# A state space, attention and feed-forward block on one core: oT's split behind the last head, half of w_out's split among the gates, four banks for two sets of transposes, and another order ahead of the state space

## Chip, core and metric

The kernel runs on one core of a Trainium2 chip. The metric is device time in microseconds (us), the median of several runs. A run of this kernel is one launch that reads all inputs from HBM and writes the whole output.

Five things work side by side on a core: TensorE (PE, matrix products and transposes into PSUM banks), VectorE (DVE), ScalarE (ACT), GpSimd (POOL), and the DMA queues, most of them filled by SyncE (SP). Each engine works through its own list in order. Semaphores tie the lists together.

## The reference, cut to what matters

One layer on 512 tokens of width 1024, in fp32:

```
n1 = rmsnorm(x, g_mix);  z = n1 @ w_in
y_ssm = s5_mixer(z[:, 0:512], ...)             # diagonal state space, 32 groups, gelu, glu
y_nsa = nsa_mixer(q = z[:, 512:1024], kv = z[:, 1024:1792], gates, ...)
merge = sigmoid(z[:, 1816:])
mixed = merge[:, :1024] * (y_ssm @ w_br_ssm) + merge[:, 1024:] * (y_nsa @ w_br_nsa)
h = x + mixed @ w_out
h = h + conv_ffn(rmsnorm(h, g_ffn), ...)
h = h + sigmoid(rmsnorm(h, g_ple) @ w_ple_gate) * (p @ w_ple_proj)
return rmsnorm(h, g_final)
```

The attention has 8 heads in two groups, each head with a compressed branch, a selected branch and a window branch.

## The kernel before, in words

**Split products.** PE takes its operands in a format that keeps fewer bits than fp32. So each fp32 operand is split into a high half and a low half: `split` (L86) copies to the high half on ACT (`copy`, L84) and subtracts on DVE or POOL (`tt`, L61). `mm3` (L90 to L93) then issues three matmuls, high by high (L91), by low (L92, L93). A weight comes by `wload` (L191): a DMA on SP into a raw buffer `wr` (three in turn), a copy `wh` on ACT, a subtraction `wl`. `wh` and `wl` have two buffers each, unless `keep` names a place of its own. In this kernel a projection of 128 columns is 24 matmuls of 128x512 (`proj`, L202; a bank `pj`).

**Transposes and banks.** `to_t` (L160) transposes a normed tile by PE (L168), four transposes to a bank, and reads each bank with ACT (the high half, L171) and DVE (the low half, `stt`, L72). Its argument `tags` says which of the PSUM banks it takes: there are two each of `acc`, `s`, `t`, `o`, and `?` stands for acc and o in turn (`either`, L180). A transpose into a bank waits until the last readers of that bank are done.

**Order.** In three parts the order is written out (`manual_schedule`); elsewhere a scheduler lays the recorded instructions out, led by the order in which the code records them and by `tc.issue_after(x)`, which holds instructions behind x.

**The state space stage.** The four projections u (columns 0 to 511 of w_in), the query projections 0 to 3 (`queries`), and four quarters of the state space (`ssm_quarter`, L725) share PE. DVE makes the tables of the state space: the powers PR and PI (L584 to L598), nr, den, kr and ki (L601 to L614), bb (L706 to L711), then for each quarter the products z (L735, with POOL making x beside them) and the scans. In the code before, PR to ki are recorded ahead of the u projections, behind `trig_at`, so that DVE's list has them between the `wl` of the second and third u weight. `wbps` (L755) are the transposes of Z, `wps` (L763) products of their result, `cps` (L634) transposes of C.

**Attention.** For 16 units (a head and a branch, L1118), `scores` makes `sps`, ACT its exponential `pr`, `transposed` (L1040) turns `pr` on PE into `ptp`, and `split` makes `ph` (ACT) and `pl` (DVE); `values` (L1049) multiplies by them into `ops`, and at the end of a head ACT copies `otmp` and DVE adds `oT`. Between them PE gets fillers (L1082): the gates (`pj` with L937's tanh) and the state space's branch products `br` with `t1b` (L1071). When the last head is done, `for _ in fill: pass` (L1134) records what is left of the fillers, some six gates. Then comes `oS`, the split of oT in four parts (L1144), w_br_nsa's products `br` from oS (L1155), `mTh` and `mTl`, and w_out: two halves of 512 columns, four loads each, `w0h`/`w0l` (POOL) and `w1h`/`w1l` (DVE) (L1172). 

**Norms 2 and 3.** The output product `wo` gives `hres`; for each pair of row tiles `to_t` makes n2h and n2l (L1202), the operands of the feed-forward products `ua` and `ub`. Behind the feed-forward part, norm 3 has two pairs too: `transposed(0, ...)` with the tags "tt??" and `transposed(1, ...)` with "tttt" (L1556), for the gating products `pg` (L1568).

Of the kernel before, what the change touches and what calls it, by code (L numbers as in the profile page):

```python
# [18 lines left out]
P = 128  # L19
# [26 lines left out]
def hybrid_kernel(ctx: ExitStack, tc: tile.TileContext, A, out):  # L46
# [36 lines left out]
    def copy(o, a):  # L83
        S.activation(o, a, AF.Copy)  # L84
# [90 lines left out]
    def last(engine):  # L175
        return next(i for i in reversed(nc.cur_bb.bb.instructions) if i.engine == engine)
# [54 lines left out]
    pP = sP.enter_context(pool("ssm_prep", 1, "right"))  # L231
    prow = pP.tile([NPAIR, 3, P], F32, name="prow")
# [3 lines left out]
    braw = pP.tile([P, 2, NPAIR, 16], F32, name="braw")  # L236
# [245 lines left out]
    with tc.manual_schedule(engines={mybir.EngineType.PE, mybir.EngineType.Activation, mybir.EngineType.DVE,  # L482
# [86 lines left out]
        trig_at = last(mybir.EngineType.DVE)  # L569
        rho_at = last(mybir.EngineType.Pool)  # L570
# [10 lines left out]


    behind = ExitStack()
    behind.enter_context(tc.issue_after(trig_at))  # L584
# [17 lines left out]
    nr, den, kr, ki = (st(n) for n in ("nr", "den", "kr", "ki"))  # L602
    ts(nr, PR[:, :, 1], -1.0, None, ADD)
    tt(den, lre, lre, MUL)
    tt(pt, aim, aim, MUL)
    tt(den, den, pt, ADD)
    V.reciprocal(den, den)
    tt(kr, nr, lre, MUL)
    tt(pt, PI[:, :, 1], aim, MUL)
    tt(kr, kr, pt, ADD)  # L610
    tt(kr, kr, den, MUL)
    tt(ki, PI[:, :, 1], lre, MUL)
    tt(pt, nr, aim, MUL)
    tt(ki, ki, pt, SUB)  # L614
    tt(ki, ki, den, MUL)
    shb = [P, NPAIR, 16]
    bt = st("bt", shb)
# [56 lines left out]
    tab_at = last(mybir.EngineType.Pool)  # L674
# [20 lines left out]
    ud = pud.tile([4, P, L, NCH], F32, name="ud")  # L695
    for ct in range(4):
        un = pw.tile([P, L, NCH], F32, name="un", tag="mg")
        copy(un, proj(ct * P, w=uw[ct] if ct < 2 else None).rearrange("p (c j) -> p j c", j=L))
        nc.sync.dma_start(ud[ct], un)
        for j in range(L):  # L700
            n = L - 1 - j
            nc.sync.dma_start(Uc[32 * n:32 * n + 32, 4 * ct:4 * ct + 4], ud[ct, :, j].rearrange("(a c) k -> c a k", c=32))


    with tc.issue_after(last(mybir.EngineType.DVE)):
        tt(bb[:, 0], braw[:, 0], krb, MUL)  # L706
        tt(bt, braw[:, 1], kib, MUL)
        tt(bb[:, 0], bb[:, 0], bt, SUB)
        tt(bb[:, 1], braw[:, 0], kib, MUL)
        tt(bt, braw[:, 1], krb, MUL)  # L710
        tt(bb[:, 1], bb[:, 1], bt, ADD)  # L711
# [11 lines left out]
    for t in SR:  # L723
        G.memset(t[:, :, 0:1], 0.0)
    def ssm_quarter(q, afters):  # L725
# [24 lines left out]

        WB = []
        for i, z in enumerate((Zr, Zi)):
            ps = bank("t", "wbps")
            for b in range(4):
                PE.transpose(ps[:, b * P:(b + 1) * P], z[:, b].rearrange("p j g c -> p (j g c)"), ident)  # L755
# [59 lines left out]
        for j in range(L):  # L815
            o = [yps[32 * b:32 * b + 32, j * NCH:(j + 1) * NCH] for b in range(4)]
            for b in range(4):
                PE.matmul(o[b], tz[:, b, 32 * j:32 * j + 32], Uc[:, 4 * q + b], start=True, stop=False)
            for x, s, last in ((Xr, sr[0], False), (Xi, sr[1], True)):
                for b in range(4):  # L820
                    PE.matmul(o[b], x[:, b, j + 1].rearrange("p g c -> p (g c)"), s[:, b], start=False, stop=last)
# [8 lines left out]
    with tc.issue_after(tab_at):  # L830
        G.tensor_copy(W2d, W2[:, 0:1].to_broadcast([P, 2, HD]))
# [3 lines left out]
    with tc.issue_after(tab_at):  # L835
        G.memset(KC.bitcast(F32), 0.0)
# [297 lines left out]
    for _ in fill:  # L1134
        pass

# [7 lines left out]
    for i in range(4):  # L1144
        split(oS[:, 0, i], oS[:, 1, i], oT[:, i])
# [23 lines left out]
    w0l = [slot(py, "y8", [P, 4, 512], F32R, "w0l0"), slot(pa, "v8", [P, 4, 512], F32R, "w0l1")]  # L1169

    w1h, w1l = (slot(p, t, [P, KD, 512], F32R, n) for p, t, n in ((po, "y16", "w1h"), (pa, "kv", "w1l")))
    for hf in range(2):  # L1172
        for c in range(4):
            ks, k4 = slice(2 * c, 2 * c + 2), slice(2 * (c % 2), 2 * (c % 2) + 2)
            keep = (w1h[:, ks], w1l[:, ks]) if hf else (w0h[:, ks], w0l[c // 2][:, k4])
            wload("w_out", D, 2 * c * P, hf * 512, 2, 512, (G, V)[hf], keep=keep)
# [14 lines left out]
    for qp in range(2):  # L1191
# [10 lines left out]
        to_t([xg[:, j] for j in range(2)], 2 * qp, 0, lambda x, k, q, w: (n2h, n2l)[x][:, k, q * P:q * P + w])  # L1202
# [142 lines left out]
    with tc.manual_schedule(engines={mybir.EngineType.PE}):  # L1345
# [210 lines left out]
        turned = transposed(1, normed(1))  # L1556
# [80 lines left out]
```

## Time and profile before

| what | us |
|---|---|
| median of 3 runs | 820.4 (820.36 to 820.62) |
| the profiled execution, its own time | 821.42 |
| its span | 819.7 |
| POOL busy, its share | 258.0 (31%) |
| DMA, mean rate over the span | 107 GB/s |

The profile is one execution, 1.0 us above the median. Its span runs from the first to the last recorded instruction, 1.7 us less than its own time. The granted clock of PE was 0.997 of full speed on average. In a timeline, a row has its start from the span's begin, its duration, engine, line, operation, `out<-in`, shape, and in brackets the idle time ahead of it with what ended it. A full-width matmul is listed with 0.39 us, but the next starts after 0.23, since matmuls overlap.

### The profile page before, as it was taken

To read this page: it belongs to the slowest core of one execution; us is meant where nothing else is said; L and a number is where in the kernel's file an instruction comes from. 1 tells how busy PE (TensorE), PEld (TensorE's weight loads), DVE (VectorE), ACT (ScalarE), POOL (GpSimd) and SP (SyncE) were. 2 spreads that over 40 slices of the span, in tenths; PEclk is the share of its full clock that TensorE was granted. 3 is DMA by queue.
4 is the path that set the end of the run, shared out by engine and by line. 5 is a ranking of instruction groups with operands and counts; after the bars stand their busy time and mean duration, and the time that the engine had idled before them with its cause. 6 is when DMAs were issued, how large, how long until landed. Compare 5 with 4: busy or idle time off the path is not lost.

```text
span 819.7 us, 12256 instructions
## 1 busy us (share of the span) xinstructions
PE 803.5 (98%) x4545; PEld 675.4 (82%) x4545; DVE 509.5 (62%) x994; ACT 398.4 (49%) x735; POOL 258.0 (31%) x321
## 2 busy tenths in 40 slices
PE   8999999999999999999999999999999999999996
PEld 7977889887888878878898888888888888888875
DVE  8796989848677730295344444455444784868753
ACT  6427454437777752335354344444443443445642
POOL 4884220005555534142032332233333210000342
PEclk9999999999999999999999999999999999999998
DMA  9955322423333422345025233333333344352111
GB/s 294 267 143 147 83 69 65 109 65 98 79 78 78 155 56 78 103 154 155 1 78 153 82 100 102 104 103 87 93 103 98 101 137 158 111 168 78 51 53 52
DMA packets 114307, 87.87 MB, mean 107 GB/s; under 512 B 9922, under 2 KB 97734, under 8 KB 114247
## 3 DMA queue, kind: packets, MB, share of 16 engines
q1 hardware_dynamic: 113572, 86.02, 36.1%
q10 hardware_dynamic: 674, 1.07, 0.4%
q8 instruction: 36, 0.59, 0.3%
q14 instruction: 25, 0.20, 0.1%
HBM read 77.63 MB, written 5.24 MB: 101 GB/s over the span
## 4 chain that ended last, share of the span: by engine, by line
PE 77%; DVE 10%; ACT 4%; issue 3%; POOL 3%; DMA 2%; SPq 0%; POOLq 0%; DVEq 0%; ACTq 0%
PE ua L92 5%; PE ua L91 5%; PE ub L92 5%; PE ua L93 5%; PE ub L91 5%; PE ub L93 5%; PE pj L91 4%; PE pj L93 4%; PE pj L92 4%; PE p L93 2%; PE p L91 2%; PE p L92 2%; PE sps L1029 2%; PE ptp L1044 2%; DVE wl L61 2%
## 5 line engine op out<-in xcount | busy, mean ns | idle before, releaser
L61 POOL TENSOR_TENSOR wl<-wr,wh 128x1024 fp32r<-128x1024 f32 x35 | 84.2, 2405 | 191.0 <-ACT wh L84 190.9
L84 ACT ACTIVATE wh<-wr 128x1024 fp32r<-128x1024 f32 x91 | 96.2, 1059 | 97.6 <-issue 31.7
L61 DVE TENSOR_TENSOR wl<-wr,wh 128x1024 fp32r<-128x1024 f32 x57 | 72.8, 1278 | 65.4 <-ACT wh L84 65.3
L91 PE MATMUL pj<-n1h,wh 128*128 128x512 f32 x224 | 91.7, 410 | 0.3 <-DVE QT L61 0.3
L93 PE MATMUL pj<-n1h,wl 128*128 128x512 f32 x224 | 88.2, 394 | 1.7 <-DVE wl L61 1.7
L92 PE MATMUL pj<-n1l,wh 128*128 128x512 f32 x224 | 87.6, 391 | 0.0
L72 DVE SCALAR_TENSOR_TENSOR cv<-ub,cvp,cv 128x511 f32<-128x511 f32 (+1 forms) x44 | 32.9, 748 | 65.1 <-ACT cv L1309 64.4
L69 POOL TENSOR_SCALAR pr<-pr,su,odds 128x512 f32<-128x512 f32 (+1 forms) x64 | 41.5, 652 | 90.4 <-DVE su L1036 76.4
L92 PE MATMUL ua<-n2l,wh 128*128 128x512 f32 (+1 forms) x176 | 67.0, 381 | 0.4 <-DVE n2l L72 0.4
L91 PE MATMUL ua<-n2h,wh 128*128 128x512 f32 (+1 forms) x176 | 66.9, 380 | 0.0
L93 PE MATMUL ub<-n2h,wl 128*128 128x512 f32 (+1 forms) x176 | 66.8, 380 | 0.0
L91 PE MATMUL ub<-n2h,wh 128*128 128x512 f32 (+1 forms) x176 | 66.8, 379 | 0.0
L92 PE MATMUL ub<-n2l,wh 128*128 128x512 f32 (+1 forms) x176 | 66.8, 379 | 0.0
L93 PE MATMUL ua<-n2h,wl 128*128 128x512 f32 (+1 forms) x176 | 66.8, 379 | 0.0
L93 PEld LDWEIGHTS pj<-n1h,wl 128*128 128x128 f32 x224 | 42.0, 188 | 11.8 <-DVE wl L61 2.8
L91 PEld LDWEIGHTS pj<-n1h,wh 128*128 128x128 f32 x224 | 42.2, 188 | 8.6 <-issue 1.0
L92 PEld LDWEIGHTS pj<-n1l,wh 128*128 128x128 f32 x224 | 42.2, 189 | 7.0
L1035 ACT ACTIVATE pr<-pr,nb 128x512 f32<-128x512 f32 (+1 forms) x64 | 36.0, 562 | 8.4 <-DVE nb L1033 7.9
L92 PEld LDWEIGHTS ua<-n2l,wh 128*128 128x128 f32 x176 | 33.1, 188 | 6.7 <-DVE n2l L72 0.6
L61 DVE TENSOR_TENSOR pl<-ptp,ph 128x128 fp32r<-128x128 f32 (+1 forms) x64 | 31.2, 489 | 11.8 <-ACT ph L84 9.4
L69 POOL TENSOR_SCALAR rv<-sums 128x1 f32<-128x1 f32 (+1 forms) x10 | 3.3, 332 | 111.5 <-DVE sums L61 99.0
L91 PEld LDWEIGHTS ub<-n2h,wh 128*128 128x128 f32 x176 | 33.1, 188 | 6.3
(482 smaller groups left out, 2049.9 us busy)
## 6 DMA issues: line engine op xcount, KB each, us to landing
wr<-in_w_up_dram SPq DMA_DIRECT2D x44, 512.0 KB, 3.9
wr<-in_w_in_dram SPq DMA_DIRECT2D x28, 512.0 KB, 3.9
b<-in_w_down_dram SPq DMA_DIRECT2D x12, 512.0 KB, 5.4
wr<-in_w_down_dram SPq DMA_DIRECT2D x10, 512.0 KB, 4.7
QQ<-QT SPq DMA_DIRECT2D x16, 256.0 KB, 3.6
wr<-in_w_out_dram SPq DMA_DIRECT2D x8, 512.0 KB, 3.5
wr<-in_w_ple_gate_dram SPq DMA_DIRECT2D x8, 512.0 KB, 3.6
xall<-in_x_dram SPq DMA_DIRECT2D x4, 512.0 KB
```

Source lines behind the costliest of these rows:

```text
L61: e.tensor_tensor(o, a, b, op=op)
L69: e.tensor_scalar(o, a, s1, s2, op0=op0, op1=op1)
L72: e.scalar_tensor_tensor(o, a, s, b, op0=op0, op1=op1)
L84: S.activation(o, a, AF.Copy)
L91: PE.matmul(ps, lh, rh, start=start, stop=False)
L92: PE.matmul(ps, lh, rl, start=False, stop=False)
L93: PE.matmul(ps, ll, rh, start=False, stop=stop)
L1029: PE.matmul(ps[:, :w], self.QQ[:, x, qt * P:(qt + 1) * P], KK[:, self.br, self.g, :w], start=x == 0, stop=x == 1)
L1035: S.activation(pp, pp, AF.Exp, bias=nb, scale=-1.0, accum_out=su)
L1044: PE.transpose(ps[:, (qt - kt) * P:(qt - kt + 1) * P], self.pr[qt][:, kt * P:(kt + 1) * P], ident)
```

## The change

It has five parts.

1. **The order ahead of the state space.** The u projections are recorded ahead of the tables. PR and PI now stand behind the `wl` of the third u weight, nr to ki behind that of the fourth; what follows (FL, the tables' products) stands behind the copies of the fourth weight. POOL's clearing of `sr` goes behind the x products of the first quarter, the copy W2d and the clearing of KC behind the second quarter's POOL work. The transposes `wbps` stand behind the second query projection.
2. **oS.** The four splits are held behind the last ACT and the last DVE instruction of the last head, and recorded ahead of the fillers that are left.
3. **w_out.** The four loads of the first half stand between those fillers, one after each 24 steps of them; their subtraction is DVE's, not POOL's.
4. **Norm 2.** The second pair's transposes take the banks "tt??".
5. **Norm 3.** The second pair's transposes take "ttss".

What this does to the lists of three places follows. The first is DVE ahead of the state space, from the end of PI's powers to bb (a piece of the difference; wl are the low halves of the weights, the rest the tables named above):

```order
 L61 TENSOR_TENSOR pt<-PI 128x16
-L61 TENSOR_TENSOR wl<-wr,wh 128x1024
 L61 TENSOR_TENSOR PR<-PR,pt 128x16
 L61 TENSOR_TENSOR pt<-PI,PR 128x16
 L61 TENSOR_TENSOR PI<-PI,pt 128x16
+L61 TENSOR_TENSOR wl<-wr,wh 128x1024
+L67 TENSOR_SCALAR nr<-PR 128x16
+L61 TENSOR_TENSOR den<-lre 128x16
 L61 TENSOR_TENSOR pt<-prm 128x16
+L61 TENSOR_TENSOR ki<-PI,lre 128x16
+L61 TENSOR_TENSOR kr<-nr,lre 128x16
```

The wl taken out is that of the third u weight, which now stands directly behind the second's, ahead of all powers. The wl put in is that of the fourth, which stood behind ki before.

The second place is ACT at the last head. Before:

```order
L84 ACTIVATE ph<-ptp 128x128
L1035 ACTIVATE pr_3842,su<-pr_3842,nb 128x256
L84 ACTIVATE oS<-oT 128x512 x3
L1035 ACTIVATE pr_3875,su<-pr_3875,nb 128x128
L84 ACTIVATE otmp<-ops 64x512
L84 ACTIVATE ph<-ptp 128x256
```

Now, behind the last head (otmp of the last head, oS, then the gates' copies wh with their tanh into t and the first w0h):

```order
L84 ACTIVATE otmp<-ops 64x512
L84 ACTIVATE oS<-oT 128x512 x4
L84 ACTIVATE wh<-wr 128x1024
L947 ACTIVATE t_3856<-pj 128x512
L84 ACTIVATE w0h<-wr 128x1024
L84 ACTIVATE wh<-wr 128x1024
```

The three splits have left the scores of the last head, where the two pr, otmp and ph now follow each other; all four stand behind the last head, and w0h among the gates' wh.

The third place is PE at norm 2's second pair (nt the transposes, ub and ua feed-forward products; what an instruction waits for in brackets). Before:

```order
L168 MATMUL nt<-ident,xg 128x128 [waits DVE_49]
L168 MATMUL nt<-ident,xg 128x128 x5
L93 MATMUL ub<-n2h,wl 128x256
L91 MATMUL ub<-n2h,wh 128x256
L92 MATMUL ub<-n2l,wh 128x256
L93 MATMUL ub<-n2h,wl 128x256
L91 MATMUL ua<-n2h,wh 128x256 [waits Activation_49]
L91 MATMUL ub<-n2h,wh 128x256
L92 MATMUL ua<-n2l,wh 128x256 [waits DVE_49]
```

Now:

```order
L168 MATMUL nt<-ident,xg 128x128 [waits DVE_49]
L168 MATMUL nt<-ident,xg 128x128 x5
L168 MATMUL nt<-ident,xg 128x128 [waits Activation_49]
L168 MATMUL nt<-ident,xg 128x128 x5
L91 MATMUL ub<-n2h,wh 128x256
L92 MATMUL ub<-n2l,wh 128x256
L93 MATMUL ub<-n2h,wl 128x256
L91 MATMUL ub<-n2h,wh 128x256
L92 MATMUL ub<-n2l,wh 128x256
L93 MATMUL ub<-n2h,wl 128x256
L91 MATMUL ua<-n2h,wh 128x256 [waits Activation_49]
L91 MATMUL ub<-n2h,wh 128x256
```

All transposes of the pair now stand in one row, with two more ub products between them and the first ua; the later two banks of transposes stood between ua products before.

The diff, cut to its core:

```diff
@@ -566 +568 @@
             if qt == 1:
                 turns()
         u_split(1, 1)
-        trig_at = last(mybir.EngineType.DVE)
-        rho_at = last(mybir.EngineType.Pool)
     first_v = last(mybir.EngineType.PE)
     nc.sync.dma_start(perow[:, 0], dr("cmp_pe_k", 0, [[P, NPAIR], [1, P]]))
     nc.sync.dma_start(perow[:, 1], dr("cmp_pe_v", 0, [[P, NPAIR], [1, P]]))
@@ -579 +579 @@
     sX.close()
+    ud = pud.tile([4, P, L, NCH], F32, name="ud")
+    uhigh, ulow = [], []
+    for ct in range(4):
+        if ct > 1:
+            uw.append(wload("w_in", INW, 0, ct * P, KD, P))
+            uhigh.append(last(mybir.EngineType.Activation))
+            ulow.append(last(mybir.EngineType.DVE))
+        un = pw.tile([P, L, NCH], F32, name="un", tag="mg")
+        copy(un, proj(ct * P, w=uw[ct]).rearrange("p (c j) -> p j c", j=L))
+        nc.sync.dma_start(ud[ct], un)
+        for j in range(L):
+            n = L - 1 - j
+            nc.sync.dma_start(Uc[32 * n:32 * n + 32, 4 * ct:4 * ct + 4], ud[ct, :, j].rearrange("(a c) k -> c a k", c=32))
     behind = ExitStack()
-    behind.enter_context(tc.issue_after(trig_at))
+    behind.enter_context(tc.issue_after(ulow[0]))
     G.memset(PR[:, :, 0:1], 1.0)
     G.memset(PI[:, :, 0:1], 0.0)
@@ -599 +612 @@
-    nr, den, kr, ki = (st(n) for n in ("nr", "den", "kr", "ki"))
...
+    nr, den = (st(n) for n in ("nr", "den"))
+    with tc.issue_after(ulow[1]):
+        ts(nr, PR[:, :, 1], -1.0, None, ADD)
+        tt(den, lre, lre, MUL)
...
+        tt(ki, ki, pt, SUB)
+        tt(ki, ki, den, MUL)
-    bt = st("bt", shb)
@@ -625 +638 @@
+    behind.enter_context(tc.issue_after(uhigh[1]))
@@ -692 +705 @@
...
-    for ct in range(4):
-        copy(un, proj(ct * P, w=uw[ct] if ct < 2 else None).rearrange("p (c j) -> p j c", j=L))
...
-    with tc.issue_after(last(mybir.EngineType.DVE)):
+    with tc.issue_after(ulow[1]):
@@ -720 +723 @@
-    for t in SR:
-        G.memset(t[:, :, 0:1], 0.0)
@@ -748 +750 @@
         powers((Zr, Zi), L, "z", PR, PI, bb[:, 0], bb[:, 1], (SUB, ADD), V, afters[0])
         powers((Xr, Xi), L + 1, "x", PR, PI, CT[:, 0], CT[:, 1], (ADD, SUB), G, afters[1])
+        if q == 0:
+            with tc.issue_after(last(mybir.EngineType.Pool)):
+                for t in SR:
+                    G.memset(t[:, :, 0:1], 0.0)
         WB = []
         for i, z in enumerate((Zr, Zi)):
             ps = bank("t", "wbps")
-            for b in range(4):
-                PE.transpose(ps[:, b * P:(b + 1) * P], z[:, b].rearrange("p j g c -> p (j g c)"), ident)
+            with tc.issue_after(turned_at):
+                for b in range(4):
+                    PE.transpose(ps[:, b * P:(b + 1) * P], z[:, b].rearrange("p j g c -> p (j g c)"), ident)
             w = mt4(f"WB{i}")
             copy(w, ps.rearrange("p (a b) -> p a b", a=4))
             WB.append(w)
@@ -827 +834 @@
-    with tc.issue_after(tab_at):
+    def w2d():
         G.tensor_copy(W2d, W2[:, 0:1].to_broadcast([P, 2, HD]))
-    with tc.issue_after(tab_at):
+    def kc0():
         G.memset(KC.bitcast(F32), 0.0)
@@ -901 +908 @@
+    turned_at = last(mybir.EngineType.PE)
@@ -912 +920 @@
             with tc.issue_after(last(mybir.EngineType.Pool)):
+                w2d()
+                kc0()
@@ -1131 +1141 @@
                     next(fill, None)
     filled(2)
     pend[0].values(pend[1], pend[2])
-    for _ in fill:
-        pass
-
+    heads_at = [last(e) for e in (mybir.EngineType.Activation, mybir.EngineType.DVE)]
     sB.close()
     pm_ = sY.enter_context(pool("mix", 1, "right"))
@@ -1141 +1149 @@
     w0h = pm_.tile([P, KD, 512], F32R, name="w0h")
     hres = slot(cp, "h16", [P, NQ, D], F32, "hres")
     oS = slot(pa, "kv", [P, 2, 4, T], F32R, "oS")
-    for i in range(4):
-        split(oS[:, 0, i], oS[:, 1, i], oT[:, i])
+    with tc.issue_after(heads_at[0]), tc.issue_after(heads_at[1]):
+        for i in range(4):
+            split(oS[:, 0, i], oS[:, 1, i], oT[:, i])
+    w0l = [slot(py, "y8", [P, 4, 512], F32R, "w0l0"), slot(pa, "v8", [P, 4, 512], F32R, "w0l1")]
+    for c in range(4):
+        for _ in range(24):
+            next(fill, None)
+        ks, k4 = slice(2 * c, 2 * c + 2), slice(2 * (c % 2), 2 * (c % 2) + 2)
+        wload("w_out", D, 2 * c * P, 0, 2, 512, V, keep=(w0h[:, ks], w0l[c // 2][:, k4]))
+    for _ in fill:
+        pass
     mTls = []
@@ -1166 +1183 @@
             for dt_ in range(2 * d2 - 2, 2 * d2 + 2):
                 split(mTh[:, dt_], mTl(dt_), t2()[:, dt_])
-    w0l = [slot(py, "y8", [P, 4, 512], F32R, "w0l0"), slot(pa, "v8", [P, 4, 512], F32R, "w0l1")]
-
     w1h, w1l = (slot(p, t, [P, KD, 512], F32R, n) for p, t, n in ((po, "y16", "w1h"), (pa, "kv", "w1l")))
-    for hf in range(2):
-        for c in range(4):
-            ks, k4 = slice(2 * c, 2 * c + 2), slice(2 * (c % 2), 2 * (c % 2) + 2)
-            keep = (w1h[:, ks], w1l[:, ks]) if hf else (w0h[:, ks], w0l[c // 2][:, k4])
-            wload("w_out", D, 2 * c * P, hf * 512, 2, 512, (G, V)[hf], keep=keep)
+    for c in range(4):
+        ks = slice(2 * c, 2 * c + 2)
+        wload("w_out", D, 2 * c * P, 512, 2, 512, V, keep=(w1h[:, ks], w1l[:, ks]))
     crow = pw.tile([44, 4, P], F32, name="crow", tag="mg")
     cvp = cp.tile([P, 4, 44], F32, name="cvp")
     for i in range(3):
@@ -1199 +1212 @@
             stt(hres[:, qt, cs], ps, 0.5, hres[:, qt, cs], MUL, ADD)
         for j in range(2):
             norm(xg[:, j], hres[:, 2 * qp + j])
-        to_t([xg[:, j] for j in range(2)], 2 * qp, 0, lambda x, k, q, w: (n2h, n2l)[x][:, k, q * P:q * P + w])
+        to_t([xg[:, j] for j in range(2)], 2 * qp, 0, lambda x, k, q, w: (n2h, n2l)[x][:, k, q * P:q * P + w],
+             tags=("tttt", "tt??")[qp])
     sY.close()
     sA.close()
@@ -1553 +1567 @@
             t.done()
         next(turned)
         norm_at = [last(e) for e in (mybir.EngineType.DVE, mybir.EngineType.Activation)]
-        turned = transposed(1, normed(1))
+        turned = transposed(1, normed(1), "ttss")
         for _ in prep:
             pass
```

More of the change, by code (lines that the diff above doesn't have):

```diff
@@ L231, in hybrid_kernel @@
     pP = sP.enter_context(pool("ssm_prep", 1, "right"))
+    braw = pP.tile([P, 2, NPAIR, 16], F32, name="braw")
+    bt = pP.tile([P, NPAIR, 16], F32, name="bt")
+    kr, ki = (pP.tile([P, NPAIR], F32, name=n) for n in ("kr", "ki"))
     prow = pP.tile([NPAIR, 3, P], F32, name="prow")
@@ L235, in hybrid_kernel @@
     perow = pP.tile([NPAIR, 2, P], F32, name="perow")
-    braw = pP.tile([P, 2, NPAIR, 16], F32, name="braw")
     craw = pP.tile([P, 2, 4, 2, HD], F32, name="craw")
@@ L599, in hybrid_kernel @@
     tt(rho4, rho4, rho4, MUL)
-    nr, den, kr, ki = (st(n) for n in ("nr", "den", "kr", "ki"))
[L603 to L615, printed above, removed]
+    nr, den = (st(n) for n in ("nr", "den"))
+    with tc.issue_after(ulow[1]):
+        ts(nr, PR[:, :, 1], -1.0, None, ADD)
+        tt(den, lre, lre, MUL)
+        tt(pt, aim, aim, MUL)
+        tt(den, den, pt, ADD)
+        V.reciprocal(den, den)
+        tt(kr, nr, lre, MUL)
+        tt(pt, PI[:, :, 1], aim, MUL)
+        tt(kr, kr, pt, ADD)
+        tt(kr, kr, den, MUL)
+        tt(ki, PI[:, :, 1], lre, MUL)
+        tt(pt, nr, aim, MUL)
+        tt(ki, ki, pt, SUB)
+        tt(ki, ki, den, MUL)
     shb = [P, NPAIR, 16]
-    bt = st("bt", shb)
     krb, kib = kr[:, :, None].to_broadcast(shb), ki[:, :, None].to_broadcast(shb)
@@ L672, in mirrored @@
                          AF.Copy, scale=sign)
-    tab_at = last(mybir.EngineType.Pool)
     maskb = pa.tile([P, T], F32, name="maskb")
@@ L692, in masks @@
         G.affine_select(out=blk, in_=blk, pattern=[[32, 4]], compare_op=ALU.is_ge, fill=0.0, base=31, channel_multiplier=-1)
-    ud = pud.tile([4, P, L, NCH], F32, name="ud")
-    for ct in range(4):
-        un = pw.tile([P, L, NCH], F32, name="un", tag="mg")
-        copy(un, proj(ct * P, w=uw[ct] if ct < 2 else None).rearrange("p (c j) -> p j c", j=L))
[L699 to L702, printed above, removed]
-    with tc.issue_after(last(mybir.EngineType.DVE)):
+    with tc.issue_after(ulow[1]):
         tt(bb[:, 0], braw[:, 0], krb, MUL)
@@ L818, in ssm_quarter @@
                 PE.matmul(o[b], tz[:, b, 32 * j:32 * j + 32], Uc[:, 4 * q + b], start=True, stop=False)
-            for x, s, last in ((Xr, sr[0], False), (Xi, sr[1], True)):
+            for x, s, fin in ((Xr, sr[0], False), (Xi, sr[1], True)):
                 for b in range(4):
-                    PE.matmul(o[b], x[:, b, j + 1].rearrange("p g c -> p (g c)"), s[:, b], start=False, stop=last)
+                    PE.matmul(o[b], x[:, b, j + 1].rearrange("p g c -> p (g c)"), s[:, b], start=False, stop=fin)
         stt(un, un, dcol[:, q:q + 1], yps, MUL, ADD)
```

## The prediction

> **What bounds the kernel now.** I read the busy times of the engines first, then the list of what TensorE (PE) waited for, then the timeline around each of those waits.
>
> ```profile
> PE 803.5 (98%) x4545; PEld 675.4 (82%) x4545; DVE 509.5 (62%) x994; ACT 398.4 (49%) x735; POOL 258.0 (31%) x321
> ```
>
> PE is busy for 803.5 us, 98% of the span, and the change takes no matmul away. It can only win back waits of PE, and what it wins goes through to the end, because everything behind is PE's work again. The columns below: who waited for what, us in total, times, longest.
>
> ```profile
> PE pj L93 <- DVE wl L61: 1.7, 3, 0.7
> PE ops L1059 <- DVE pl L61: 0.9, 1, 0.9
> PE nt L168 <- DVE n L72: 0.7, 2, 0.5
> PE ops L1058 <- ACT ph L84: 0.5, 1, 0.5
> PE ua L92 <- DVE n2l L72: 0.4, 1, 0.4
> PE wo L91 <- DVE t L72: 0.3, 1, 0.3
> PE pj L91 <- DVE QT L61: 0.3, 1, 0.3
> PE wbps L755 <- ACT Z L84: 0.2, 1, 0.2
> ```
>
> These lines lie at places that the change touches: pj and wbps in the state space stage (five waits, 2.2 us), ops at the last head (1.4), wo at the output projection (0.3), ua at norm 2 (0.4), nt at norm 3 (0.7). The list's other lines, at the start, at the first scores and in the feed-forward part, belong to code that keeps its order, and I leave them as they are. A listed gap understates its loss, because matmuls overlap. The rows of PE's timeline (start, duration, and in brackets the gap and what ended it) show it:
>
> ```profile
> 290.07 0.39 PE L93 MATMUL pj<-n1h,wl 128*128 128x512 f32 x1
> 290.98 0.39 PE L1058 MATMUL ops<-ph,VV 128*128 128x256 f32 x1 [0.53 <-ACT ph L84]
> 292.27 0.39 PE L1059 MATMUL ops<-pl,VV 128*128 128x256 f32 x1 [0.90 <-DVE pl L61]
> 784.29 0.39 PE L92 MATMUL pg<-wg1l,n 128*128 128x512 f32 x1
> 784.51 0.39 PE L93 MATMUL pg<-wg1h,n 128*128 128x512 f32 x1
> 785.40 0.63 PE L168 MATMUL nt<-ident,xn 128*128 128x128 f32 x4 [0.50 <-DVE n L72]
> 786.19 0.63 PE L168 MATMUL nt<-ident,xn 128*128 128x128 f32 x4 [0.16 <-DVE n L72]
> ```
>
> Full-width matmuls start 0.22 to 0.23 us apart (784.29, 784.51). From 784.51 to 785.40 are 0.89, so 0.66 is lost where the gap says 0.50; at 290.98 it is 0.68 for 0.53. I add 0.16 to each gap. The pair at the last head I count by starts: 0.68, and 1.29 less 0.12 (half a full width) or 1.17, so 1.85.
>
> **State space order.** Five gaps of 2.2 us make 2.2 + 5 x 0.16 = 3.0 us at stake. What decides is whether VectorE (DVE) has each weight's low half, wl, in time. Its list before runs from the end of the second u weight to the second query weight:
>
> ```profile
> L84 ACT ACTIVATE wh<-wr 128x1024 fp32r<-128x1024 f32 x91 | 96.2, 1059 | 97.6 <-issue 31.7
> 43.59 0.39 PE L93 MATMUL pj<-n1h,wl 128*128 128x512 f32 x1
> 63.15 0.41 DVE L61 TENSOR_TENSOR z<-PR,bb 128x256 f32<-128x256 f32 x1
> 66.25 1.22 DVE L61 TENSOR_TENSOR wl<-wr,wh 128x1024 fp32r<-128x1024 f32 x1
> 43.08:67.47 24.39, 22.49 (x97) 17.46 (x97) 22.46 (x59) 9.82 (x20) 15.29 (x38) 1.00 0.61 160
> ```
>
> In that window (busy: PE, PEld, DVE, ACT, POOL) DVE works 22.46 us in 59 instructions: four wl, 39 small ones on 128x16, six bb and ten z. The change keeps the list but for its order, and three of the z move behind it: 22.46 - 3 x 0.41 = 21.2. The list can start when the third u weight's high half is there. Its buffer is free when PE leaves the first projection (the row at 43.59 is already the second), about 43.5, and the copy takes 1.06: 44.6. So DVE ends the list at 65.8, or 66.2 with what little idle time its dependences leave. PE wants the second query weight's low half four projections after the same place of the second u projection at 43.59: 4 x 24 x 0.227 = 21.8, and 0.4 for four transposes, so 65.8. The two u weights, now first, are early (the third ready at 45.8, wanted near 49); the first query weight comes close to its need. So 0.4 of stall stays at the second query weight, and I allow 0.4 more where the third query projection waits for the bank that the first one's copies free. That leaves 0.8 of 3.0 and gives **2.2** (bounds: 1.2, if the first query weight stalls by 1.0 too, and 3.0). The wbps transposes now stand behind the second query projection, where their Z are long ready, and the copies that the last listed bank waits for stand ahead of the scans, so these two waits go. What else moves is far from its reader: the clearing of sr and KC and the copy W2d on POOL go behind the x products, tens of us ahead of their use, and the u rows' DMAs leave SP in their old order.
>
> The order also splits the last gelu from its companions: two more table loads on ScalarE (ACT), ahead of the third block's exponential.
>
> ```profile
> 154.63 2.18 ACT L84 ACTIVATE ys<-yT 128x512 fp32r<-128x512 f32 x4
> 156.83 1.28 ACT L956 ACT_TABLE_LOAD   x1
> 171.29 0.42 DVE L61 TENSOR_TENSOR cmps<-cmps,csu 128x256 f32<-128x256 f32 x1
> 175.25 0.38 PE L968 MATMUL pct<-ident,cmps 128*128 128x128 f32 x2
> ```
>
> A load costs 1.28, directly behind the splits. The block that this exponential feeds is ready at 171.71 and wanted at 175.25: 3.5 us of cover, of which the two loads take at most 2.6. I cost them at nothing; without cover they cost up to 2.6. The Trainium skill (ScalarE: Activation LUTs, What ACT_TABLE_LOAD costs) gives 2.66 us for a switch, a drain of 1.38 included; by it the two would take 5.3 and lose 1.8, and the sum below would be 3.55. The trace does not bear the drain out: only 0.02 us lie between the splits' end at 156.81 and the load.
>
> **oS behind the last head.** ACT, then DVE, around the two ops waits:
>
> ```profile
> 287.84 1.68 ACT L84 ACTIVATE oS<-oT 128x512 fp32r<-128x512 f32 x3
> 289.42 0.39 ACT L1035 ACTIVATE pr<-pr,nb 128x128 f32<-128x128 f32 x1
> 289.93 0.59 ACT L84 ACTIVATE otmp<-ops 64x512 f32<-64x512 f32 x1
> 290.55 0.38 ACT L84 ACTIVATE ph<-ptp 128x256 fp32r<-128x256 f32 x1
> 288.51 1.52 DVE L61 TENSOR_TENSOR oS<-oT,oS 128x512 fp32r<-128x512 f32 x2 [0.18 <-ACT oS L84]
> 289.95 0.67 DVE L72 SCALAR_TENSOR_TENSOR t1b<-t1b,br 128x512 f32<-128x512 f32 x1
> 291.23 0.66 DVE L61 TENSOR_TENSOR oT<-ops,otmp 64x512 f32<-64x512 f32 x1
> 291.81 1.03 DVE L61 TENSOR_TENSOR pl<-ptp,ph 128x256 fp32r<-128x256 f32 x2
> ```
>
> On ACT three splits of oT stand ahead of pr, otmp and ph, 1.68 us together. Without them ACT is free at 287.84; the three take 0.39 + 0.59 + 0.38 and some 0.2 for reading out a sum, 1.6, so ph is ready near 289.8 even if pr's scores come 0.4 later. PE wants it at 290.07 + 0.23 = 290.3: the 0.68 goes. On DVE the splits go too, but t1b still waits for its branch product, some instructions ahead of the row at 290.07 on PE; I put it at 289.35, between 288.51, where the splits began, and its old 289.95. Then comes oT, until 290.6, and pl until 291.05; PE wants that at 290.3 + 0.12 = 290.42. So 0.6 of the 1.17 stays, and the next thing late is oT. Gain **1.2** (bounds 0.7, if ph of the next step, behind a weight copy of 1.06, becomes late; and 1.85). The four splits then stand near 309, where their readers come 30 us later.
>
> **w_out's first half.** Its low halves go from GpSimd (POOL) to DVE, about 30 us earlier.
>
> ```profile
> 354.35 6.91 DVE L61 TENSOR_TENSOR mTl<-t,mTh 128x512 fp32r<-128x512 f32 x4
> 355.07 8.44 POOL L61 TENSOR_TENSOR w0l<-wr,w0h 128x1024 fp32r<-128x1024 f32 x3 [5.91 <-ACT w0h L84]
> 335.36 1.23 DVE L61 TENSOR_TENSOR wl<-wr,wh 128x1024 fp32r<-128x1024 f32 x1 [22.10 <-ACT wh L84]
> 329.96 2.39 POOL L61 TENSOR_TENSOR wl<-wr,wh 128x1024 fp32r<-128x1024 f32 x1 [3.05 <-ACT wh L84]
> wr<-in_w_br_nsa_dram SPq DMA_DIRECT2D x4, 512.0 KB, 3.4
> 339.68 0.39 PE L91 MATMUL br<-oS,wh 128*128 128x512 f32 x1
> ```
>
> Beside POOL's splits, four mTl take 6.91 us of DVE; two of their size took 1.52 above, so four take 3.0, and 3.9 come free ahead of the products that wo's bank waits for: that wait goes, 0.3 + 0.16 = **0.45** (bounds 0 and 0.6, should other waits be as near). The four splits of 1.23 on DVE lie in its idle 22.10 us. The four high halves on ACT lie between the gates' copies, which wait for PE anyway. The price is in SP's queue: four loads now stand among those of the gates, on three raw buffers. The first branch weight gets the buffer that POOL frees at 332.35; with 3.4 of load and 1.06 of copy it is ready at 336.8, wanted at 339.68. The cover is 2.9 us, and each us beyond it PE waits.
>
> **Norms.** At norm 2 PE ran out of work before the first ua product that needs n2l (0.4 + 0.16). Six more transposes (four took 0.63 above) and two more ub products of half width (0.12 each) now stand ahead of it, more than is lost; the two banks that they need come from acc and o, and stt of hres, their last reader, is done before the norm that feeds the transposes. **0.5** (0 to 0.55). At norm 3 the transposes go to two free banks: 0.66, and 0.16 + 0.16, **1.0** (0.3 if the gating's n copies then come late; they have 12 products of cover, 2.7 us).
>
> **Sum.** 2.2 + 1.2 + 0.45 + 0.5 + 1.0 = 5.35. The profiled execution took 821.4 us (span 819.7) and would take 816.1; the median, 1.0 below it, goes from 820.4 to 815.0. Nothing that PE does later is bound elsewhere, except the tail behind its last product, which moves with it.
>
> **Rivals.** *DVE stays late* (0.16): it is at 22.46 of 24.39, and PE, arriving sooner, waits at the query weights and banks instead. The state space gain falls to 0.5: 816.7. For it: how near 66.2 and 65.8 are; against it: two of the five waits are at u weights that are now 3 us early. *The banks only move the wait* (0.10): both norms give nothing, as the copies behind the transposes are late next: 815.0 + 1.5 = 816.5. Against it: the covers named. *The table loads reach the path* (0.03): each holds ACT for two loads' time, so 5.1 against a cover of 3.5, and 1.6 is lost: 816.6. The Trainium skill (ScalarE: Activation LUTs, What ACT_TABLE_LOAD costs) speaks for it; the 0.02 us after the splits speak against it. *Most of it returns* (0.11): the state space keeps 0.5, oS 0.7, norm 3 its 0.3, the others nothing: 820.4 - 1.5 = 818.9. *Slower* (0.05): the regrouped list meets POOL's tables, and each of its 39 small operations costs 0.3 more, as one did here:
>
> ```profile
> 53.02 0.68 DVE L61 TENSOR_TENSOR kr<-kr,pt 128x16 f32<-128x16 f32 x1
> ```
>
> The list is then 21.2 + 11.7 = 32.9 and ends at 77.5, the stall is 11.7 instead of 3.0, and with the other gains of 3.15 the time is 820.4 + 8.7 - 3.15 = 825.9. It turns slower than before once the stall passes 6.15, the list 27.4. Against it: POOL was 15.29 busy in that window before, so the 22.46 already holds such meetings, and the average operation was much shorter.
>
> **Numbers.** My forecast has 0.55. Within 0.2% (1.6 us), which is about what a measurement of this kernel can tell from no change, lies the case in which most of the gain returns, 0.11; faster by more are the forecast and the three rivals near 816.6, 0.84 together; the slower one has 0.05. The range reaches from all upper bounds, 3.0 + 1.85 + 0.6 + 0.55 + 1.0 = 7.0 or 813.4, to just above the case in which most returns, 819.0.
>
> **What would show it.** The waits list of PE: nt, ua and wo gone; ops at 0.6 in one row of pl; pj near 0.8; four mTl near 3 us. I am wrong if pj still waits over 2 us, if new rows appear for br after the gates, or if oS splits delay the gates.

## The result, and the profile after

The changed kernel takes **813.33 us** (median of 4 runs, 813.15 to 813.41) beside 820.38 for the kernel before on the same chip: a ratio of 0.9912, with a 95% interval from 0.9898 to 0.9926. The gain is 7.05 us where 5.35 were forecast. The time lies 0.07 below the low end of the range, 813.4.

The busy times of the profiled execution of the changed kernel (its own time 813.41, span 811.6) and the first five of the seven lines in its list of PE's waits (us in total, times, longest):

```profile
PE 800.8 (99%) x4545; PEld 676.0 (83%) x4545; DVE 508.0 (63%) x998; ACT 400.9 (49%) x737; POOL 248.6 (31%) x317
```

```profile
PE gb L491 <- DVE ones L247: 1.1, 1, 1.1
PE sps L1039 <- DVE nb L1043: 0.7, 2, 0.5
PE ops L1069 <- DVE pl L61: 0.4, 1, 0.4
PE ptr L387 <- DMA pin<-in_p_dram: 0.3, 1, 0.3
PE pj L93 <- DVE wl L61: 0.2, 1, 0.2
```

PE has the same 4545 matmuls, 2.7 us less of busy time, and a span 8.1 shorter (more than the 7.05 between the medians, since the profiled execution of before was 1.0 above its median). The rows of nt L168, ua, wo, wbps and of the bank (pj L91) are gone; of ops one row is left instead of two, and of pj's three waits for wl one, of 0.2. Of the waits that the prediction hoped to remove, that is all that remains.

**Where it was won** is read from the same PE instruction in both traces: how much earlier does it start? Five places cut the program into stages. These are the rows of before: the first u product, the first scores, a gate in the last head, behind its waits, the last product of w_out, the first down projection, and PE's last matmul.

```profile
37.10 0.48 PE L91 MATMUL pj<-n1h,wh 128*128 128x512 f32 x1
...
185.93 0.61 PE L1029 MATMUL sps<-KK,QQ 128*128 128x512 f32 x2
...
300.01 0.48 PE L91 MATMUL pj<-n1h,wh 128*128 128x512 f32 x1
...
407.60 0.39 PE L93 MATMUL wo<-w1h,mTl 128*128 128x512 f32 x1
...
650.89 0.39 PE L91 MATMUL dn<-wh,ffp 128*128 128x512 f32 x1
...
811.37 0.28 PE L93 MATMUL pg<-wg1h,n 128*128 128x256 f32 x1
```

The same instructions in the changed kernel:

```profile
36.79 0.50 PE L91 MATMUL pj<-n1h,wh 128*128 128x512 f32 x1
...
182.39 0.39 PE L1039 MATMUL sps<-KK,QQ 128*128 128x512 f32 x1
...
295.13 0.48 PE L91 MATMUL pj<-n1h,wh 128*128 128x512 f32 x1
...
401.74 0.39 PE L93 MATMUL wo<-w1h,mTl 128*128 128x512 f32 x1
...
644.36 0.39 PE L91 MATMUL dn<-wh,ffp 128*128 128x512 f32 x1
...
803.55 0.28 PE L93 MATMUL pg<-wg1h,n 128*128 128x256 f32 x1
```

They start 0.31, 3.54, 4.88, 5.86, 6.53 and 7.82 earlier. The differences between neighbours are what each stage gave: state space 3.23, last head 1.34, w_out 0.98, norm 2 0.67, and 1.29 in the last stage. Of these 1.29, 0.22 comes at one down projection that the change does not touch, and 1.07 at norm 3. The first 0.31 lies ahead of the change.

### The profile page after: what moved, and what is told of

Same layout as the page of the kernel before. It is cut to its first block, busy times and chain, and to the rows that moved or that the text cites. A ratio compares the mean times of both kernels' runs of the same rounds, so it can differ in the third digit from the quotient of the medians.

```text
span 811.6 us, 12255 instructions
## 1 busy us (share of the span) xinstructions
PE 800.8 (99%) x4545; PEld 676.0 (83%) x4545; DVE 508.0 (63%) x998; ACT 400.9 (49%) x737; POOL 248.6 (31%) x317
## 3 DMA queue, kind: packets, MB, share of 16 engines
q10 hardware_dynamic: 674, 1.07, 0.4%
## 4 chain that ended last, share of the span: by engine, by line
PE 91%; DVE 5%; DMA 1%; ACT 1%; issue 1%; SPq 0%; POOLq 0%; POOL 0%; ACTq 0%; DVEq 0%
PE pj L91 5%; PE pj L93 5%; PE pj L92 5%; PE ub L91 5%; PE ua L91 5%; PE ua L92 5%; PE ub L93 5%; PE ua L93 5%; PE ub L92 5%; PE p L93 2%; PE p L91 2%; PE p L92 2%; PE dn L92 2%; PE dn L93 2%; PE dn L91 2%; PE sps L1039 2%
## 5 line engine op out<-in xcount | busy, mean ns | idle before, releaser
L91 PE MATMUL pj<-n1h,wh 128*128 128x512 f32 x224 | 91.3, 408 | 0.0
L91 PE MATMUL ua<-n2h,wh 128*128 128x512 f32 (+1 forms) x176 | 66.9, 380 | 0.0
L91 PE MATMUL ub<-n2h,wh 128*128 128x512 f32 (+1 forms) x176 | 66.9, 380 | 0.0
L91 PEld LDWEIGHTS pj<-n1h,wh 128*128 128x128 f32 x224 | 42.2, 188 | 7.9 <-issue 0.4
L93 PEld LDWEIGHTS ua<-n2h,wl 128*128 128x128 f32 x176 | 33.1, 188 | 6.3
L92 PEld LDWEIGHTS ub<-n2l,wh 128*128 128x128 f32 x176 | 33.2, 188 | 6.2
L93 PEld LDWEIGHTS ub<-n2h,wl 128*128 128x128 f32 x176 | 33.1, 188 | 6.2
```

Of the source, the lines that this page charges most:

```text
L91: PE.matmul(ps, lh, rh, start=start, stop=False)
L92: PE.matmul(ps, lh, rl, start=False, stop=False)
L93: PE.matmul(ps, ll, rh, start=False, stop=stop)
```

## The experiments

Theory and rival come from one look at the rows around a wait. This is the first u weight that PE waited for in the kernel before; PEld are the weight loads:

```profile
48.83 0.39 PE L92 MATMUL pj<-n1l,wh 128*128 128x512 f32 x1
49.95 0.19 PEld L93 LDWEIGHTS pj<-n1h,wl 128*128 128x128 f32 x1 [1.16 <-DVE wl L61]
49.95 0.50 PE L93 MATMUL pj<-n1h,wl 128*128 128x512 f32 x1 [0.74 <-DVE wl L61]
50.06 0.19 PEld L91 LDWEIGHTS pj<-n1h,wh 128*128 128x128 f32 x1
50.29 0.39 PE L91 MATMUL pj<-n1h,wh 128*128 128x512 f32 x1
...
50.52 0.39 PE L92 MATMUL pj<-n1l,wh 128*128 128x512 f32 x1
```

From 48.83 to 49.95 are 1.12 instead of 0.23: 0.90 lost for a gap of 0.74, the 0.16 of the prediction. But the waiting matmul then lasts 0.50 instead of 0.39, and the next one starts 0.34 behind it instead of 0.23. That is another 0.11, outside the pair of rows on which the prediction had measured its price. **Theory:** a wait ahead of a full-width matmul costs its gap and 0.27, so five waits were 3.64 (counted by starts) and not 3.0, and the gain is what the starts above say. **Rival one:** the prediction's terms were right, and the rest came from places outside the change, the start, the down projection and the tail. **Rival two**, for the rest of the chain: PE's stall is not set by DVE's list.

**Each part undone by itself** (four kernels on one chip, where the kernel before took 820.77, 0.4 more than beside the changed kernel). The state space order of before, all its hunks reversed, among them:

```diff
-    behind.enter_context(tc.issue_after(ulow[0]))
+    behind.enter_context(tc.issue_after(trig_at))
```

> The changed kernel with the state space order of before; oS, w_out and both norms stay changed. My theory now: a wait of PE ahead of a full-width matmul costs its gap and 0.27 more, 0.16 at the wait itself and 0.11 behind it, as the next weight is not loaded ahead; so five waits came to 3.6, not 3.0, and this part is worth 3.3, what PE's starts differ by at the end of the stage. Then this kernel takes 813.3 + 3.3 = 816.6. Rival, the price of the prediction (gap and 0.16, part worth 2.2): 815.5, and the rest of the gain came from elsewhere. The five waits of before should be back in the list, 2.2 us, and the row behind each should start 0.33 to 0.35 after it instead of 0.23.

Measured: 816.76 (816.25 to 817.17), ratio 0.9947 (0.9935 to 0.9960). The time is the theory's 816.6 and not 815.5. The first u product starts at 37.15 and the first scores at 185.95, 0.36 and 3.56 later than in the changed kernel: 3.20 in this stage. The waits are back:

```profile
PE pj L93 <- DVE wl L61: 1.7, 3, 0.7
...
PE pj L91 <- DVE QT L61: 0.3, 1, 0.3
PE wbps L755 <- ACT Z L84: 0.2, 1, 0.2
```

The four splits of oS, not held:

```diff
-    with tc.issue_after(heads_at[0]), tc.issue_after(heads_at[1]):
-        for i in range(4):
-            split(oS[:, 0, i], oS[:, 1, i], oT[:, i])
+    for i in range(4):
+        split(oS[:, 0, i], oS[:, 1, i], oT[:, i])
```

> The changed kernel with the four splits of oS not held: they stand amid the last head again. My theory: the part is worth 1.33, so 814.65. The prediction's 1.2 gives 814.5; its upper bound of 1.85, 815.2. The two cannot be told apart by time; the waits of ops can: 0.5 and 0.9 again in place of one of 0.4.

Measured: 815.28 (814.91 to 816.30). By time alone this is the 815.2 of the prediction's upper bound, 0.6 above the theory. But PE's starts differ by 1.34 across the last head; the rest is that the profiled run, the median one, also started 0.26 later and lost 0.3 at a down projection, as other runs of untouched code do (below). Both waits of ops are back:

```profile
PE ops L1069 <- DVE pl L61: 0.9, 1, 0.9
...
PE ops L1068 <- ACT ph L84: 0.5, 1, 0.5
```

w_out's first half as before (the eight loads in one loop again, the first four subtracted by G):

```diff
-    wload("w_out", D, 2 * c * P, 0, 2, 512, V, keep=(w0h[:, ks], w0l[c // 2][:, k4]))
+    wload("w_out", D, 2 * c * P, hf * 512, 2, 512, (G, V)[hf], keep=keep)
```

> The changed kernel with w_out's first half as before: its loads behind the mixing, its low halves on POOL; oS stays held. My theory: the part is worth 0.98, by a listed wait of 0.3 and several smaller ones at the same products, so 814.3. Prediction: worth 0.45, so 813.8. The four mTl should take near 6.9 us again.

Measured: 814.23 (814.12 to 815.29). The starts differ by 0.73, between the prediction's 0.45 and the 0.98 of the two main traces. DVE's low halves of the mixed product last 6.89 again, and 2.49 in the changed kernel. First this kernel, then the changed one:

```profile
349.42 6.89 DVE L61 TENSOR_TENSOR mTl<-t,mTh 128x512 fp32r<-128x512 f32 x4
```

```profile
348.34 2.49 DVE L61 TENSOR_TENSOR mTl<-t,mTh 128x512 fp32r<-128x512 f32 x4
```

The old banks at both norms (both tag arguments taken out):

```diff
-             tags=("tttt", "tt??")[qp])
...
-        turned = transposed(1, normed(1), "ttss")
+        turned = transposed(1, normed(1))
```

> The changed kernel with the old banks at norms 2 and 3. My theory: worth 0.67 + 1.07 = 1.74, so 815.05. Prediction: 1.5, so 814.8. Rival: the whole 0.75 that PE's starts differ by at the start, at the down projections and in the tail belongs to the change; then the four parts undone one by one come to 6.3 and less where they overlap, and none of these kernels gives it back.

Measured: 815.71 (815.00 to 816.01), 0.66 above the theory; its profiled run began 0.39 later than the changed kernel's. The starts differ by 0.66 at norm 2 and 1.11 at norm 3, and both waits are back:

```profile
PE nt L168 <- DVE n L72: 0.7, 2, 0.5
...
PE ua L92 <- DVE n2l L72: 0.4, 1, 0.4
```

By PE's starts the four kernels give back 3.20 + 1.34 + 0.73 + 0.66 + 1.11 = 7.04, against 7.05 between the medians. That the two agree to 0.01 is luck, given how far medians of the same code lie apart (below), but nothing near the 1.7 that rival one needs is left.

**The changed kernel once more**, beside the next three:

> The changed kernel itself, once more, beside the next three on the same chip: 813.3, and 7.0 below the kernel before (ratio 0.991). If PE's starts at the start of the program or at the down projections differ from the first run of the same code by 0.2 or more, these differences are none of the change's.

Measured: 813.58 (813.12 to 814.01), 820.63 before on this chip, ratio 0.9907 (0.9894 to 0.9921). Its first u product starts at 36.56, where the first run of the same code had 36.79; in the kernels below and above, with the same code up to there, it starts between 36.66 and 38.30. So the start of the program differs from run to run by some tenths, once by 1.7. The stretch from the first down projection to the last, 54.46 here, takes 54.25 to 54.99 in the other kernels, with the same code there. So rival one falls for good. The kernel before had medians from 820.38 to 821.01 on the four chips of this study: a difference of less than 0.6 between medians of different chips tells nothing.

**The hold of wbps taken away**, the order of the tables kept:

```diff
-            with tc.issue_after(turned_at):
-                for b in range(4):
-                    PE.transpose(ps[:, b * P:(b + 1) * P], z[:, b].rearrange("p j g c -> p (j g c)"), ident)
+            for b in range(4):
+                PE.transpose(ps[:, b * P:(b + 1) * P], z[:, b].rearrange("p j g c -> p (j g c)"), ident)
```

> The changed kernel without the rule that holds the wbps transposes behind the second query projection; the order of the tables stays. My theory: VectorE's new order carries most of the 3.3 of this stage, and the placing of wbps what its wait and the bank's wait (0.2 and 0.3, each with 0.27) cost: up to 1.0, so 813.7 to 814.3. Rival: the placing is worth nothing, since other copies hold the bank anyway: 813.3.

Measured: 813.60 (813.41 to 813.84), not to be told from 813.58. PE's starts show a small cost: 0.06 earlier at the first u product, 0.26 later at the first scores, so 0.32. One wait for the bank is there instead:

```profile
PE pj L91 <- DVE QT L61: 0.6, 1, 0.6
```

So the place of the transposes carries 0.3 of the 3.2, and 2.9 is left for the rest of this part. That this is the order of DVE's list above all is argued from the waits for wl that came back when the part was undone (1.7 of 2.2 listed); what moved on POOL was not undone by itself.

**More work in DVE's list**, seven multiplications ahead of the first query weight's low half (the second hunk holds that low half behind them):

```diff
-        tt(bt, braw[:, 1], kib, MUL)
+        for _ in range(8):
+            tt(bt, braw[:, 1], kib, MUL)
...
+            with tc.issue_after(held.pop()):
+                tt(lo, raw, hi, SUB, e)
```

> The changed kernel with seven more multiplications of 128x256 in VectorE's list ahead of the first query weight's low half (one product of bt made eight times; the result is the same). They start 0.34 apart, 2.4 in all. My theory: VectorE's list has no room left, so PE stalls for each us of it, and a second wait brings its 0.27: 813.3 + 2.4 + 0.3 = 816.0, with pj listed with two waits, 2.2 to 2.8 together. Rival: the list has idle time or the stall is given back behind the query projections, where PE is ahead of VectorE: 813.3 to 814.5.

Measured: 816.86 (816.53 to 817.00). Rival two falls, but 0.9 more is lost than the theory allows. The waits are one instead of two, and what follows it is new:

```profile
62.42 0.80 PE L93 MATMUL pj<-n1h,wl 128*128 128x512 f32 x1 [2.21 <-DVE wl L61]
63.02 0.63 PE L91 MATMUL pj<-n1h,wh 128*128 128x512 f32 x1
63.45 0.63 PE L92 MATMUL pj<-n1l,wh 128*128 128x512 f32 x1
...
65.93 0.40 PE L92 MATMUL pj<-n1l,wh 128*128 128x512 f32 x1
66.16 0.39 PE L93 MATMUL pj<-n1h,wl 128*128 128x512 f32 x1
```

Behind the wait, full-width matmuls start 0.43 apart until 65.93, and 0.23 apart from then on. The granted clock says why; in the table by stretches the busy times of PE, PEld, DVE, ACT and POOL are followed by the clock, the DMA share and GB/s:

```profile
60.20:62.30 2.10, 0.02 (x1) 0.00 (x0) 2.03 (x5) 2.08 (x6) 0.00 (x0) 1.00 0.12 34
62.42:65.83 3.41, 3.41 (x8) 2.74 (x9) 3.38 (x5) 0.38 (x2) 2.37 (x3) 0.50 0.70 146
66.00:70.00 4.00, 4.00 (x19) 3.31 (x18) 3.35 (x7) 2.78 (x7) 2.55 (x4) 1.00 0.94 299
```

For 3.41 us PE ran at half its clock. The wait cost 2.37, the matmul behind it 0.37, six more 0.20 each and one 0.12: 4.06 for a gap of 2.21, 1.6 more than gap and 0.27. The same with four and with twelve multiplications (range(5) and range(13)):

> As the kernel with seven more multiplications, but with four, 1.02 less: the wait at the first query weight should have a gap of 1.2 instead of 2.2. Behind the gap of 2.2 PE's full-width matmuls started 0.43 apart for some 3 us, instead of 0.23, and that cost 1.6 more; behind the longest gap of the kernel before, 0.9, they did not. Theory one: the slow stretch comes of long gaps only (nearer 2 than 1), so this kernel takes 813.5 + 1.35 + 0.11 - 0.48 (the second query weight's wait, which goes) = 814.5. Theory two: any gap over 1 brings it: 816.0. If instead the slow starts come from VectorE's extra operations and not from the gap, some of them should remain here too.

> As before, with twelve more multiplications: 5 x 0.34 = 1.7 more than with seven, a gap of 3.9. If the slow stretch behind the wait has a fixed length: 816.9 + 1.7 = 818.6. If it grows with the gap: 820.0 or more. This is also what the slower rival of the prediction was: a list that ends 4.1 later, priced there at 1 us of PE for each us of list alone, which from the changed kernel gives 813.4 + 4.1 + 0.3 - 0.5 = 817.3.

Measured: 814.75 (814.43 to 816.11) with four, 819.42 (818.24 to 820.47) with twelve. (The kernel before took 821.01 on this chip.) The gap with four came out at 0.79, not 1.2: in these kernels the added products start 0.46 apart, not 0.34, but the low half, held, stands one product earlier than in the changed kernel, and there it had been done 0.48 before its matmul (at 59.41, the matmul at 59.89). So DVE's list had some room after all, and the near match of gap and forecast with seven, 2.2 and 2.4, was luck. With four, PE is at full speed right behind the gap:

```profile
62.37 0.50 PE L93 MATMUL pj<-n1h,wl 128*128 128x512 f32 x1 [0.79 <-DVE wl L61]
62.71 0.40 PE L91 MATMUL pj<-n1h,wh 128*128 128x512 f32 x1
62.94 0.40 PE L92 MATMUL pj<-n1l,wh 128*128 128x512 f32 x1
```

This wait costs 0.95 and 0.11, the theory's gap and 0.27, at a weight for which the changed kernel does not wait. With twelve the gap is 4.53, and the clock stays down for longer. It falls while PE still waits, at 62.97, and PE works at half clock from 64.58 to 69.80:

```profile
60.00:62.97 2.97, 0.05 (x1) 0.00 (x0) 2.73 (x8) 2.60 (x7) 0.00 (x0) 1.00 0.29 86
62.97:64.58 1.61, 0.00 (x0) 0.00 (x0) 1.61 (x3) 0.00 (x0) 0.00 (x0) 0.50 0.03 9
64.58:69.80 5.22, 5.22 (x12) 4.13 (x13) 5.08 (x9) 1.13 (x3) 3.13 (x5) 0.50 0.84 224
```

From 62.97 to 69.80 are 6.83 us, twice the 3.41 of the kernel with seven.

With four, the extra work is there and the half clock is not; that it comes of the gap is argued from the two gaps over 2. It begins somewhere between a gap of 0.90 or 0.91 (ops in the kernel before and in the two kernels with oS undone, where the clock stayed up) and one of 2.21. In the profiled runs it costs 1.6 behind 2.21 and 2.4 behind 4.53 (there 0.37, ten of 0.20 and 0.17, less the 0.11).

The median with twelve lies between the two forms of its expectation, because each fits a part of the eleven runs. Four took 820.04 to 820.47 at a mean granted clock of 0.993, the profiled one among them; seven took 818.24 to 819.45 at 0.995 or 0.996, around the 818.6 of a fixed length. By an estimate from these figures, a mean clock lower by 0.002 over 818 us means some 3.3 us more at half clock, about one stretch of 3.41, so the seven probably had one stretch where the four had two. No profile of the seven was kept, and what decides between one and two stays open. The 817.3 of the price without the clock lies below every run.

**Two and three waits less**, the theory turned into a kernel. At the last head but one, pl goes ahead of oT on DVE; z of the second quarter goes behind the second query weight's wl; in the second kernel ScalarE also copies QT ahead of the second quarter's Z:

```diff
+            if add:
+                with tc.issue_after(last(mybir.EngineType.DVE)):
+                    add()
...
+        with tc.issue_after(low_at[1] if q else first_v):
             powers((Zr, Zi), L, "z", PR, PI, bb[:, 0], bb[:, 1], (SUB, ADD), V, afters[0])
...
-        ssm_quarter(q, high_at[-2:])
+        ssm_quarter(q, (qt_at[0], high_at[-1]) if q == 1 else high_at[-2:])
```

> The changed kernel with two more steps of the same sort: z of the second quarter behind the low half of the second query weight, and at the last head but one pl ahead of oT on VectorE. Both remaining waits (gaps of 0.20 and 0.38) should go. My theory, each gap with 0.27 more: 0.48 and 0.53 (at half width), 1.0 together, so 812.3. The price of the prediction, each gap with 0.16: 0.36 + 0.54 = 0.9, so 812.4. Rival: the next thing is late at once, ph behind the copy of a weight or oT's own reader, and nothing is gained: 813.3.

> The kernel with two waits less, and one more edit: ScalarE copies QT of the first query projection ahead of Z of the second quarter, since PE then waited 0.26 + 0.11 for the bank that QT's split frees. Theory: 812.76 - 0.35 = 812.4. Rival: the next thing late takes its place: 812.8.

Measured: 812.76 (812.67 to 812.81) and 812.88 (812.42 to 813.50). The first is 0.82 below the changed kernel on the same chip, with no run in common: the lowest median of the study, ratio 0.9897 (0.9884 to 0.9911) to the kernel before. Both waits went, by 0.45 and 0.59 in PE's starts, and the rival came true in part: at the third query projection PE, arriving sooner, now waits for the bank. The row shows no gap in brackets, only the 0.50 of a weight that was not loaded ahead:

```profile
71.34 0.50 PE L91 MATMUL pj<-n1h,wh 128*128 128x512 f32 x1
```

The second kernel removes that too: between the first u product and the last gate it gains 1.16 on the changed kernel, the first one 0.72. Its time does not show this: it ran on the chip where the kernel before took 821.01 instead of 820.63, and its profiled run started 0.40 later than the changed kernel's.

**Both oS and w_out undone**, to find w_out's missing 0.25:

> The changed kernel with oS and w_out's first half both as before. PE's starts differ between before and after by 1.33 at the last head and 0.98 at w_out; undone alone they gave 1.34 and 0.73. Theory: w_out's remaining 0.25 hangs on both parts (waits at its second half that each part alone removes), so together they give 2.3: 813.45 + 2.3 = 815.75. Rival: 0.25 is a difference between runs: 2.07, so 815.5. The time cannot tell these two apart, PE's starts can.

Measured: 816.32 (815.95 to 817.50); the profiled run began 0.77 later than the changed kernel's. PE's starts give 1.33 at the last head and 0.77 at w_out, 2.10: the two parts add up, and the theory of a joint effect falls. The rest of the 0.98 is a wait at w_out's second half (0.17) and a slightly longer first one in the profile of before; none of the other kernels has the former. Whether it belongs to that run or to the parts together stays open.

## Why the prediction fell short, point by point

- **The mechanism was right.** PE was the bound, each part removed the waits it was said to remove, and all of it reached the end. No rival of the prediction happened: no stall came back, no table load reached the path (pct is not in the list of waits), no branch weight was late.
- **The step that failed is "I add 0.16 to each gap".** It was measured up to the start of the waiting matmul and left out the 0.11 behind it, so a wait ahead of a full-width matmul cost its gap and 0.27. The terms of the state space, w_out and the norms were made with it, and so were their upper bounds, so the range's low end was too high as well. State space: five waits were 3.64, not 3.0. Norm 2: 0.54 and 0.10 behind it, and 0.66 to 0.67 by starts, where 0.5, at most 0.55, stood. Norm 3: 1.07 to 1.11 for 1.0.
- **What the price explains.** Of the 1.7 by which the gain was larger than forecast, the price makes about 1.0: 0.64 in the state space, 0.13 at w_out, 0.16 at norm 2, 0.07 at norm 3. The terms below make 0.6 more: 0.33 of a stall that stayed away, 0.15 of a stall that the list does not have, 0.13 at oS. That the time fell just outside the range is a matter of 0.07, and the second median of the same code, 813.58, lies inside; that each term came out larger is not luck.
- **"That leaves 0.8" was 0.47.** The stall at the second query weight was foreseen at 0.4 and is 0.36 with 0.11 behind it; the 0.4 for the bank did not come. How near that was shows in the kernel with two waits less, where it came. The rows of the changed kernel:

```profile
65.12 0.39 PE L92 MATMUL pj<-n1l,wh 128*128 128x512 f32 x1
...
65.70 0.50 PE L93 MATMUL pj<-n1h,wl 128*128 128x512 f32 x1 [0.20 <-DVE wl L61]
...
66.04 0.40 PE L91 MATMUL pj<-n1h,wh 128*128 128x512 f32 x1
```

So the term of 2.2 is 3.2: 0.64 from the price and 0.33 from the stall that stayed away. DVE's list itself was met: forecast to end at 65.8 to 66.2, it ended at 65.65, with 21.55 us of work.

```profile
42.70:65.65 22.95, 22.81 (x104) 18.47 (x102) 21.55 (x57) 10.09 (x22) 15.68 (x34) 1.00 0.63 174
```

- **w_out: 0.45 was 0.73 to 0.98.** Behind the listed gap of 0.31 there were 0.47 and 0.11, and a second stall of 0.15 that the list does not have, since its row shows no gap: a matmul of 0.50 among those of 0.39.

```profile
361.91 0.50 PE L91 MATMUL wo<-w0h,mTh 128*128 128x512 f32 x1 [0.31 <-DVE t L72]
...
364.78 0.50 PE L91 MATMUL wo<-w0h,mTh 128*128 128x512 f32 x1
365.11 0.39 PE L92 MATMUL wo<-w0l,mTh 128*128 128x512 f32 x1
```

- **oS: 1.2 was 1.33 to 1.34.** The step was right to the instruction: "the next thing late is oT". DVE in the changed kernel, and the wait that is left:

```profile
286.34 0.68 DVE L61 TENSOR_TENSOR oT<-ops,otmp 64x512 f32<-64x512 f32 x1
286.94 0.41 DVE L61 TENSOR_TENSOR pl<-ptp,ph 128x256 fp32r<-128x256 f32 x1
```

```profile
287.40 0.39 PE L1069 MATMUL ops<-pl,VV 128*128 128x256 f32 x1 [0.38 <-DVE pl L61]
```

- **The slower rival was priced too low.** It took a stall of 11.7 for 11.7 lost. The doses show that behind a gap of over 2 us PE also loses 1.6 to 2.4 to its clock, so the point from which the change would have turned slower lies lower by about that much.

## What to carry to other kernels

The price of a wait is read over three starts, not two: from the last matmul ahead of the gap to the second one behind it, less what these steps take elsewhere. In a kernel whose PE is 98% busy, look for rows with a longer duration than their neighbours as well as for gaps, since a stall of 0.1 to 0.2 has no entry in the list of waits (0.15 at wo above). And an upper bound made with the same price as the forecast is no bound: it has to be made with another row.

## What the runs showed of the hardware

- A weight that waits is not loaded ahead. In the rows above, weight load and matmul start together at 49.95, where a load else starts some 0.23 ahead of its own matmul (50.06 for the one at 50.29). The Trainium skill (TensorE: Matmul & The Clock Gate, Architectural detail: the array is 16× 32×32, not 1× 128×128) says that PE's queue can pull weight loads ahead of matmuls in flight; the rows agree. Where the load could not be pulled ahead, the waiting matmul was listed with 0.50 instead of 0.39 and the next one started 0.11 later. That the load is the cause is argued from these rows; no run took it apart.
- PE's clock fell to 0.50 of full speed at a gap of 2.21 us, for 3.41 us, and at one of 4.53, for 6.83; at gaps of 0.79 and 0.90 it did not. The Trainium skill (TensorE: Matmul & The Clock Gate, Part 1: The HAM clock gate (the "warmup" mystery)) has the clock halved after an idle window of about 3.4 us; here a gap of 2.21 was enough.
- VectorE's subtractions into mTl took 2.49 us for four in the changed kernel, where POOL was idle meanwhile, and 6.89 for the same four with w_out's part undone, where POOL was busy with w0l for 6.25 of them. Two of the four took 0.68 there and two 2.88, as long as one of POOL's subtractions (2.84 to 2.90).
